# A transformer stack on one core: four plain inner tiles per feed-forward stage instead of six, and the paired blocks' input operands in another order and partly on GpSimd

## The chip, the cores and the metric

The kernel runs on one core of one Trainium2 chip. The metric is the device time of one execution in microseconds (us); the kernel before has a median of 1789.67 us over 3 runs (1787.99 to 1789.96). TensorE (PE) multiplies, VectorE (DVE), ScalarE (ACT) and GpSimd (POOL) work on tiles in SBUF, and SP issues the loads.

## What is computed

The reference runs a convolution layer, an attention layer and then one larger block on a sequence of 512 tokens with 1024 channels, all in float32. The change touches only the two feed-forward stages of the larger block (the "passes" below, one before its mixer and one after):

```python
def swiglu_ffn(x, g, w_gate, w_up, w_down):
    h = rms_norm_2(x, g)                      # x * rsqrt(mean(x*x) + eps) * g
    return (jax.nn.silu(h @ w_gate) * (h @ w_up)) @ w_down
x = x + 0.5 * swiglu_ffn(...)                 # D_MODEL = 1024, D_FF = 2816
```

## The kernel before

**Numbers.** Activations lie transposed: 8 tiles of 128 channels by 512 tokens (`k.xT`). Each float32 matrix is split into a rounded part ("hi", made on ScalarE) and a rest ("lo", the difference, made on VectorE or GpSimd), and a product is three matmuls: hi by hi, hi by lo, lo by hi. `mm3` (L262) does this, on L264 to L266. One `mm3` followed by one `tick()` is the unit of pacing.

**Weights.** `Stream` loads 512 KB granules in the order of use through 4 raw buffers (`RBUFS`), splits them into 6 pairs of hi and lo buffers (`WBUFS`), and does so as far ahead as buffers allow (`fill`, after each `done`). L100 makes the hi on ScalarE; L102 the rest, on GpSimd for the keys in `POOL_MORE` (L510) and for most parts of the sums below, on VectorE otherwise.

**The norm.** The 1/rms factor of a token isn't known when the first product starts. The products run on the tiles times gain, and the evictions from PSUM multiply by `rB`, the factor broadcast over all partitions. `Norm.stats1` (L361) sums the squares with small matmuls (L365), a short chain over VectorE and GpSimd makes four diagonal tiles (L392), and `stats2` spreads them by matmuls (L403) and copies the result to SBUF on ScalarE (L405). `a_group` calls it after k = `STATS_AT` = 4 of the 8 contraction steps, and `stats2` is put off by `STATS` = 6 ticks.

**The feed-forward stage** (`ffn`, L1513). Its 22 inner tiles of 128 columns fall into parts of 6, 4, 6 and 6, each followed later by its share of the down product. The first `FFN_PLAIN` = 6 inner tiles are plain: 8 `mm3` of 512 columns for the gate and 8 for the up matrix. Tiles 0 and 1 go first, as one group of four products with the contraction outermost; `e1` evicts (L1525, L1528) and applies SiLU, `e2` multiplies and splits (L1536, L279). The other tiles go in pairs: `seven` (L1599) computes a pair's product with seven half-size products of 256 columns in place of eight, from sums and differences of weight quarters (`split_sums`, L104: L117, L118, L126, L127) and of input quarters, and puts the results together with additions (L1615). `two` does this for gate and up.

**The input's operands.** `turn_x` (L1566) makes the seven input operands for the pairs, each in two halves j: it scales the input by gain and `rB` into quarters b11, b12, b21, b22 (L1578, sixteen instructions of 256 columns), takes the differences t1 = b12 - b11, t2 = b22 - t1, t3 = b22 - b12 and t4 = t2 - b21 (L1584, L1585, L1589, L1590), and splits all seven with `split_into` (hi on ScalarE L278, rest on VectorE L279). `seven` reads them in the order b11, b21, t2, t1, t3, b22, t4. `turn_x` is a side job: `tick()` gives it `TURN_RATE` = 0.5 units, and it gives up units at each `yield`; it is added after the first group, waits for `rB`, and must be through before the first pair.

**Order.** Each engine runs its instructions in one order, which is fixed when the program is built: a list scheduler takes instructions by their place in the program, and later ones earlier where the first aren't ready by its own reckoning.

## Time and profile before

| | |
|---|---|
| median of 3 runs | 1789.67 us |
| profiled execution: time, span | 1790.32 us, 1788.4 us |
| TensorE busy, of the span | 1750.5 us, 98% |
| VectorE, ScalarE, GpSimd busy | 1268.3 us, 892.3 us, 646.3 us |
| matmuls of 512 and of 256 columns on each of L264, L265 and L266 (inputs by streamed weights) | 1344 and 896 |
| granted TensorE clock, mean | 0.991 |

A busy time counts an instruction from its start to its end, waiting for a shared resource included; it is not work done. A matmul's recorded length overlaps the next one's, so its pace is read from starts. An engine's idle time is marked in a timeline in brackets, with what ended it.

### The profile page before, as it was taken

Reading aid. Unit: us, or ns where it says so; the run is one execution under the profiler, and the core shown is the slowest. Engines: PE = TensorE matmul, PEld = TensorE weight load, DVE = VectorE, ACT = ScalarE, POOL = GpSimd, SP = SyncE. Lnnn points to the kernel's source line nnn. Section 1 sums busy time; section 2 is a strip of 40 time slices with the busy share of each in tenths; the row PEclk is TensorE's granted clock in tenths of the full one; section 3 lists DMA queues with packets and bytes.
Section 4 is the critical chain, followed back from the end, with each engine's and each line's share of the span. In section 5 each row is a group of like instructions: output and inputs, shape, how many; then the busy total and the mean of one; then the engine's idle time right before and its main releaser. Section 6 shows DMA issues by size and latency. Waiting matters only on the chain.

```text
span 1788.4 us, 25274 instructions
## 1 busy us (share of the span) xinstructions
PE 1750.5 (98%) x9468; PEld 1488.6 (83%) x9468; DVE 1268.3 (71%) x2380; ACT 892.3 (50%) x1551; POOL 646.3 (36%) x418
## 2 busy tenths in 40 slices
PE   7999799999999999999999999899999999999999
PEld 5877588888888888889999888678888888899897
DVE  5999777565466667977676659997446569777872
ACT  5777545384636544434343435667643325344441
POOL 3999410302020003466675501000000044666662
PEclk8999899999999999999999999999999999999999
DMA  6422233131322232242342533113133321433432
GB/s 180 118 83 83 59 95 95 49 99 54 97 82 73 70 94 76 61 124 84 106 128 79 157 105 106 36 47 95 59 116 97 94 80 48 121 95 95 130 88 66
DMA packets 262758, 162.14 MB, mean 91 GB/s; under 512 B 10256, under 2 KB 245100, under 8 KB 262636
## 3 DMA queue, kind: packets, MB, share of 16 engines
q1 hardware_dynamic: 262636, 160.53, 30.8%
q8 instruction: 74, 1.21, 0.3%
q14 instruction: 48, 0.39, 0.1%
HBM read 155.23 MB, written 5.28 MB: 90 GB/s over the span
## 4 chain that ended last, share of the span: by engine, by line
PE 86%; DVE 2%; ACT 1%; issue 0%; POOL 0%; ACTq 0%; POOLq 0%
PE b L265 26%; PE b L264 26%; PE b L266 26%; PE b L1271 1%; PE b L1328 1%; PE b L1914 1%; PE b L1308 1%; PE b L1215 1%; PE b L2110 0%; PE b L1898 0%; PE b L1044 0%; PE b L1045 0%; PE b L403 0%; DVE wlo L102 0%; PE b L365 0%
## 5 line engine op out<-in xcount | busy, mean ns | idle before, releaser
L265 PE MATMUL b<-s,whi 128*128 128x512 f32 (+1 forms) x2240 | 789.5, 352 | 0.2
L264 PE MATMUL b<-s,whi 128*128 128x512 f32 (+1 forms) x2240 | 786.7, 353 | 2.5 <-ACT s L623 1.3
L266 PE MATMUL b<-s,wlo 128*128 128x512 f32 (+1 forms) x2240 | 786.9, 351 | 0.0
L102 POOL TENSOR_TENSOR wlo<-raw,whi 128x1024 fp32r<-128x1024 f32 (+2 forms) x163 | 337.7, 2088 | 420.5 <-ACT whi L100 382.4
L264 PEld LDWEIGHTS b<-s,whi 128*128 128x128 f32 x2240 | 422.9, 189 | 64.2 <-ACT s L860 2.2
L265 PEld LDWEIGHTS b<-s,whi 128*128 128x128 f32 x2240 | 423.1, 189 | 62.7 <-issue 2.4
L266 PEld LDWEIGHTS b<-s,wlo 128*128 128x128 f32 x2240 | 423.0, 189 | 61.1 <-issue 1.4
L100 ACT ACTIVATE whi<-raw 128x1024 fp32r<-128x1024 f32 (+2 forms) x304 | 285.3, 950 | 355.4 <-PE b L265 207.2
L102 DVE TENSOR_TENSOR wlo<-raw,whi 128x1024 fp32r<-128x1024 f32 (+1 forms) x141 | 179.5, 1277 | 38.9 <-ACT whi L100 32.3
L264 PE MATMUL b<-whi,s 128*128 128x512 f32 (+1 forms) x416 | 172.1, 415 | 0.0
L265 PE MATMUL b<-wlo,s 128*128 128x512 f32 (+1 forms) x416 | 168.6, 406 | 0.0
L266 PE MATMUL b<-whi,s 128*128 128x512 f32 (+1 forms) x416 | 164.6, 396 | 0.0
L100 ACT ACTIVATE whi<-s 128x512 fp32r<-128x512 f32 x128 | 77.2, 627 | 153.6 <-DVE s L127 74.0
L702 POOL TENSOR_TENSOR s<-s,s 128x512 f32<-128x512 f32 x88 | 128.3, 1489 | 3.2 <-ACT s L698 2.1
L1615 DVE TENSOR_TENSOR s<-b,s 128x256 f32<-128x256 f32 x192 | 76.1, 419 | 42.4 <-PE b L266 21.5
L102 POOL TENSOR_TENSOR wlo<-s,whi 128x512 fp32r<-128x512 f32 x64 | 98.2, 1555 | 20.8 <-ACT whi L100 15.2
L704 DVE SCALAR_TENSOR_TENSOR b<-s,s,b 128x512 f32<-128x512 f32 x144 | 99.9, 749 | 3.7 <-ACT b L692 2.9
L259 POOL TENSOR_TENSOR h8y<-hv,mhalf 128x8 f32<-128x8 f32 x28 | 47.4, 1694 | 131.4 <-DVE hv L1061 113.9
L279 DVE TENSOR_TENSOR s<-s,s 128x512 fp32r<-128x512 f32 x84 | 87.5, 1064 | 5.9 <-ACT s L278 5.6
L266 PEld LDWEIGHTS b<-whi,s 128*128 128x128 f32 x416 | 79.2, 190 | 13.9
L264 PEld LDWEIGHTS b<-whi,s 128*128 128x128 f32 x416 | 79.2, 190 | 12.4 <-ACT s L1837 0.2
L265 PEld LDWEIGHTS b<-wlo,s 128*128 128x128 f32 x416 | 79.2, 191 | 10.9
(434 smaller groups left out, 2086.6 us busy)
## 6 DMA issues: line engine op xcount, KB each, us to landing
raw<-in_ffn_w_gate SPq DMA_DIRECT2D x44, 512.0 KB
raw<-in_ffn_w_up SPq DMA_DIRECT2D x44, 512.0 KB
raw<-in_attn_w_in SPq DMA_DIRECT2D x40, 512.0 KB
raw<-in_ffn_w_down SPq DMA_DIRECT2D x48, 384.0 KB
raw<-in_w_in SPq DMA_DIRECT2D x36, 512.0 KB
raw<-in_conv_w_in SPq DMA_DIRECT2D x24, 512.0 KB
raw<-in_ple_w_gate SPq DMA_DIRECT2D x16, 512.0 KB
raw<-in_conv_w_out SPq DMA_DIRECT2D x8, 512.0 KB
```

The source lines that it names most:

```text
L100: self.last_hi = self.k.nc.scalar.activation(hi, src, AF.Copy)
L102: eng.tensor_tensor(lo, src, hi.bitcast(F32), OP.subtract)
L259: self.nc.gpsimd.tensor_tensor(y, v, self.mhalf[:, :shape], OP.pow)
L264: mm(ps, a[0], b[0], start=first, stop=False)
L265: mm(ps, a[0], b[1], start=False, stop=False)
L266: self.last = mm(ps, a[1], b[0], start=False, stop=last)
L279: nc.vector.tensor_tensor(lo, src, hi.bitcast(F32), OP.subtract)
L702: nc.gpsimd.tensor_tensor(acc2, acc2, p, OP.add)
L704: nc.vector.scalar_tensor_tensor(acc, y[:, t:t + S], wcol(t, c), acc, OP.mult, OP.add)
L1215: nc.tensor.transpose(pt[:, j * 128:(j + 1) * 128], w[:, j * 128:(j + 1) * 128], k.ident)
L1271: nc.tensor.matmul(ps[:, i * w + kb * 128:i * w + kb * 128 + 128], Q[g, b][:, hc], kk[h % 2][:, hc], start=True, stop=True)
L1615: add = lambda out, p, q, op=OP.add: V.tensor_tensor(out, p, q, op)
```

## The change

The plain inner tiles are 4 instead of 6, so that each pass has nine pairs instead of eight, and the first pair comes right after tiles 0 to 3. `a_group` takes the step after which it calls its hook, and `ffn` passes 3 instead of 4; the second half of the norm's statistics is put off by 4 ticks instead of 6 there. `turn_x` is added before the first group instead of after it, with a rate of 0.55, and goes in the order in which `seven` reads: b11 and b21 of both halves first, then t1 and t2, then t3, b22 and t4. A new `split_x` makes the rests of b11, b21, b22 and t4 on GpSimd; those of t1, t2 and t3 stay on VectorE. `POOL_MORE` follows `FFN_PLAIN`: of the plain tiles, the weights of 2 and 3 have their rests on GpSimd, where it was 2 to 5.

```diff
--- before.py
+++ after.py
@@ -306,7 +306,7 @@
         assert k == nk
         return ps
 
-    def a_group(self, X, keys, hook=None):
+    def a_group(self, X, keys, hook=None, at=None):
 
         pss = [self.ps.get() for _ in keys]
         gs = [self.W.take(kk) for kk in keys]
@@ -315,7 +315,7 @@
             for ps, g in zip(pss, gs):
                 self.mm3(ps, self.wpart(g, k * 128), X[k], k == 0, k == nk - 1)
                 self.tick()
-            if hook and k == STATS_AT:
+            if hook and k == (STATS_AT if at is None else at):
                 hook()
         for g in gs:
             self.W.done(g)
@@ -372,9 +372,9 @@
         self.dg = diagonals(k, self.r4)
         k.behind = self.k.last_diag
 
-    def stats(self):
+    def stats(self, n=None):
         self.stats1()
-        self.k.defer(STATS, self.stats2)
+        self.k.defer(n or STATS, self.stats2)
 
     def stats2(self):
         self.rB = self.k.spread(self.r4, self.dg)
@@ -471,7 +471,7 @@
 
 
 FFN_PARTS = (6, 4, 6, 6)
-FFN_PLAIN = 6
+FFN_PLAIN = 4
 
 
 def ffn_order():
@@ -1502,6 +1502,8 @@
 X_ACT, X_DVE = 4, 6
 STATS = 6
 STATS_AT = 4
+STATS_FFN = 4
+STATS_FFN_AT = 3
 TURN = 9
 TURN_M = 10
 LAG = (1, 3, 5)
@@ -1568,31 +1570,56 @@
 
         while not hasattr(nm, "rB"):
             yield 0.2
+        q = {}
+
+        def quarter(kh, th, j):
+            t = q[kh, th, j] = mem.get()
+            for e in range(2):
+                n = 4 * kh + 2 * j + e
+                V.scalar_tensor_tensor(t[:, e * 256:(e + 1) * 256], k.xT[n][:, th * 256:(th + 1) * 256],
+                                       k.col(nm.gain, nm.at + n), nm.rB[:, th * 256:(th + 1) * 256], OP.mult, OP.mult)
+
+        for kh in range(2):
+            for j in range(2):
+                quarter(kh, 0, j)
+                TX[("b11", "b21")[kh], j] = split_x(q[kh, 0, j])
+                yield 0.9
+        t1, t2 = {}, {}
         for j in range(2):
-            q = {}
-            for kh in range(2):
-                for th in range(2):
-                    t = q[kh, th] = mem.get()
-                    for e in range(2):
-                        n = 4 * kh + 2 * j + e
-                        V.scalar_tensor_tensor(t[:, e * 256:(e + 1) * 256], k.xT[n][:, th * 256:(th + 1) * 256],
-                                               k.col(nm.gain, nm.at + n), nm.rB[:, th * 256:(th + 1) * 256],
-                                               OP.mult, OP.mult)
-                    yield 0.8
-            b11, b12, b21, b22 = (q[x] for x in ((0, 0), (0, 1), (1, 0), (1, 1)))
-            t1, t2 = mem.get(), mem.get()
-            V.tensor_tensor(t1, b12, b11, OP.subtract)
-            V.tensor_tensor(t2, b22, t1, OP.subtract)
-            yield 1.4
-            TX["t2", j] = k.split_into(t2)
+            quarter(0, 1, j)
+            yield 0.8
+            t1[j] = mem.get()
+            V.tensor_tensor(t1[j], q[0, 1, j], q[0, 0, j], OP.subtract)
+            mem.put(q.pop((0, 0, j)))
             yield 0.7
+            quarter(1, 1, j)
+            yield 0.8
+            t2[j] = mem.get()
+            V.tensor_tensor(t2[j], q[1, 1, j], t1[j], OP.subtract)
+            yield 0.7
+            TX["t2", j] = k.split_into(t2[j])
+            yield 0.7
+            TX["t1", j] = k.split_into(t1[j])
+            mem.put(t1[j])
+            yield 0.7
+        for j in range(2):
+            b12, b21, b22 = (q.pop((*x, j)) for x in ((0, 1), (1, 0), (1, 1)))
             V.tensor_tensor(b12, b22, b12, OP.subtract)
-            V.tensor_tensor(t2, t2, b21, OP.subtract)
-            yield 1.4
-            for name, t in (("b11", b11), ("b21", b21), ("t1", t1), ("t3", b12), ("b22", b22), ("t4", t2)):
-                TX[name, j] = k.split_into(t)
-                mem.put(t)
-                yield 0.7
+            yield 0.7
+            TX["t3", j] = k.split_into(b12)
+            TX["b22", j] = split_x(b22)
+            yield 0.8
+            V.tensor_tensor(t2[j], t2[j], b21, OP.subtract)
+            TX["t4", j] = split_x(t2[j])
+            mem.put(b12, b21, b22, t2[j])
+            yield 0.8
+
+    def split_x(t):
+
+        hi, lo = mem.get(F32R), mem.get(F32R)
+        nc.scalar.activation(hi, t, AF.Copy)
+        nc.gpsimd.tensor_tensor(lo, t, hi.bitcast(F32), OP.subtract)
+        return hi, lo
 
     halves2 = slice(0, 256), slice(256, 512)
 
@@ -1695,10 +1722,11 @@
                 mem.put(nm.rB)
             two(j)
         elif i == 0:
-            p4 = k.a_group(X, [("fg", l, 0), ("fu", l, 0), ("fg", l, 1), ("fu", l, 1)], nm.stats)
+            turn = k.add_side(turn_x(), TURN_RATE)
+            p4 = k.a_group(X, [("fg", l, 0), ("fu", l, 0), ("fg", l, 1), ("fu", l, 1)],
+                           lambda: nm.stats(STATS_FFN), STATS_FFN_AT)
             k.defer(0, lambda: e1(0, p4[0], p4[1]))
             k.defer(0, lambda: e1(1, p4[2], p4[3]))
-            turn = k.add_side(turn_x(), TURN_RATE)
             i += 1
         else:
             pg = k.a_tile(X, ("fg", l, j))
@@ -1707,7 +1735,7 @@
         i += 1
 
 
-TURN_RATE = 0.5
+TURN_RATE = 0.55
```

## Rows read from the trace of the kernel before

**Rows 1.** The page: engine totals, and by line the chain that ended last.

```profile
PE 1750.5 (98%) x9468; PEld 1488.6 (83%) x9468; DVE 1268.3 (71%) x2380; ACT 892.3 (50%) x1551; POOL 646.3 (36%) x418
...
PE b L265 26%; PE b L264 26%; PE b L266 26%; PE b L1271 1%; PE b L1328 1%; PE b L1914 1%; PE b L1308 1%; PE b L1215 1%; PE b L2110 0%; PE b L1898 0%; PE b L1044 0%; PE b L1045 0%; PE b L403 0%; DVE wlo L102 0%; PE b L365 0%
```

**Rows 2.** Stages of the first pass: stretch, length, busy PE PEld DVE ACT POOL, clock, DMA.

```profile
683.00:752.50 69.50, 69.50 (x307) 56.15 (x307) 57.20 (x79) 29.37 (x44) 27.16 (x11) 1.00 0.23 65
752.50:772.30 19.80, 19.80 (x170) 19.80 (x169) 15.58 (x24) 10.86 (x19) 12.03 (x7) 1.00 0.23 68
868.00:927.40 59.40, 59.40 (x505) 59.40 (x504) 44.63 (x77) 28.61 (x50) 38.51 (x24) 1.00 0.34 97
```

**Rows 3.** The same view, from the scale's arrival to the last operand, both passes.

```profile
706.40:753.00 46.60, 46.60 (x203) 37.46 (x202) 46.55 (x61) 22.90 (x34) 22.92 (x9) 1.00 0.27 76
1451.50:1500.40 48.90, 48.90 (x221) 39.76 (x221) 48.81 (x61) 23.76 (x36) 25.47 (x10) 1.00 0.25 73
```

**Rows 4.** TensorE's timeline at stage borders: start, length, line, operands. Both passes.

```profile
705.50 0.48 PE L265 MATMUL b<-s,whi 128*128 128x512 f32 x1
...
752.48 0.28 PE L264 MATMUL b<-s,whi 128*128 128x256 f32 x1
...
772.29 0.39 PE L264 MATMUL b<-s,whi 128*128 128x512 f32 x1
...
1450.53 0.48 PE L266 MATMUL b<-s,wlo 128*128 128x512 f32 x1
...
1497.86 0.28 PE L264 MATMUL b<-s,whi 128*128 128x256 f32 x1
...
1517.75 0.39 PE L264 MATMUL b<-s,whi 128*128 128x512 f32 x1
```

**Rows 5.** VectorE's timeline: last sums of squares, and the last operand split.

```profile
693.22 0.68 DVE L358 TENSOR_TENSOR s<-s,s 128x512 f32<-128x512 f32 x1
...
752.98 0.68 DVE L279 TENSOR_TENSOR s<-s,s 128x512 fp32r<-128x512 f32 x1
...
1432.80 0.68 DVE L358 TENSOR_TENSOR s<-s,s 128x512 f32<-128x512 f32 x1
```

**Rows 6.** Timelines of TensorE and ScalarE around the norm's scale.

```profile
698.56 0.48 PE L266 MATMUL b<-s,wlo 128*128 128x512 f32 x1
...
704.69 1.05 PE L403 MATMUL b<-diag,ones 128*128 128x128 f32 x8
...
705.78 0.60 ACT L405 ACTIVATE s<-b 128x512 f32<-128x512 f32 x1 [0.25 <-PE b L403]
...
711.08 0.61 ACT L278 ACTIVATE s<-s 128x512 fp32r<-128x512 f32 x1
...
1450.94 0.58 ACT L405 ACTIVATE s<-b 128x512 f32<-128x512 f32 x1
```

**Rows 7.** Timelines of VectorE and GpSimd in the plain stage.

```profile
705.61 10.05 POOL L102 TENSOR_TENSOR wlo<-raw,whi 128x1024 fp32r<-128x1024 f32 x4 [5.62 <-ACT whi L100]
...
707.02 0.68 DVE L1528 TENSOR_TENSOR s<-b,s 128x512 f32<-128x512 f32 x1
707.62 8.72 DVE L1578 SCALAR_TENSOR_TENSOR s<-s,pc,s 128x256 f32<-128x256 f32 x5
...
716.86 2.45 DVE L1578 SCALAR_TENSOR_TENSOR s<-s,pc,s 128x256 f32<-128x256 f32 x6
...
719.82 2.74 POOL L102 TENSOR_TENSOR wlo<-raw,whi 128x1024 fp32r<-128x1024 f32 x1 [4.16 <-ACT whi L100]
719.83 3.01 DVE L1578 SCALAR_TENSOR_TENSOR s<-s,pc,s 128x256 f32<-128x256 f32 x2
...
735.20 1.88 DVE L279 TENSOR_TENSOR s<-s,s 128x512 fp32r<-128x512 f32 x3
```

**Rows 8.** Rests on GpSimd, by line: durations ns min/median/max. First 684 us; 845 to 927.

```profile
L102 POOL TENSOR_TENSOR wlo<-raw,whi x20: 2343/2414/2864, 15.0 to 678.8; 128x1024 fp32r<-128x1024 f32 x20
...
L102 POOL TENSOR_TENSOR wlo<-s,whi x12: 1281/1298/1752, 857.9 to 915.5; 128x512 fp32r<-128x512 f32 x12
```

## The prediction

> **What bounds the kernel now.** I read the engine totals and the chain that ended last, then the stages of the feed-forward passes, then the engines that feed TensorE there. TensorE is busy 98% and the chain runs over its three split-product lines, 26% each [rows 1]. In the pass it is busy for every microsecond of each stage, at a granted clock of 1.00, the 2.4 GHz level [rows 2]; so a matmul that goes is time that goes, as long as nothing new makes TensorE wait. In the plain stage VectorE is nearly as full: from the moment the norm's scale arrives until the last operand of the paired blocks is split it is busy 46.55 of 46.6 us, and 48.81 of 48.9 in the second pass [rows 3]. That is a second bound, just hidden: its last split of an operand starts at 752.98, and the block that multiplies these operands starts at 752.48 [rows 4, 5].
>
> **Fewer matmuls: the gain.** Two plain tiles are 2 tiles x 2 matrices x 8 x 3 = 96 matmuls of 512 columns. From 705.50 to 752.48 stand 9 + 192 = 201 of them, so 46.98/201 = 0.2337 us each and 22.44 for the 96; a paired block (2 x 7 x 4 x 3 = 168 matmuls of 256 columns) ran from 752.48 to 772.29 = 19.81 [rows 4]. Gain 2.63. In the second pass 47.33/202 x 96 = 22.49 against 19.89: 2.60 [rows 4]. Together 5.2 us. That is the whole prize: steady blocks are already TensorE-bound (three in a row take 59.4 us, TensorE busy 59.40 [rows 2]). Weight traffic I cost at nothing: each of the 22 tiles still loads two 512 KB granules through the same four raw buffers, SP only issues some sooner, and in three blocks in a row no load held TensorE up; the one place without that cover is the new block's second half, whose loads must follow tile 3's splits by 710 and are wanted some 30 us later.
>
> **The scale sooner.** The sum of squares is taken after k = 3, not 4: four times three matmuls, 12 x 0.234 = 2.8 us. The data allow it: the last square is added at 693.22, the statistics' matmuls end by 698.56 and would end by 695.8; in the second pass the last square is 18 us ahead of the scale [rows 5, 6]. The shorter deferral (4 ticks for 6, 1.4 us by its count) I cost at nothing: 6 ticks are 18 matmuls, yet 26 stand between statistics and broadcast (698.56 to 704.69 [rows 6]), so the written deferral isn't what places it. At most it gives 1.4 us more. So the scale stands at 706.38 - 2.8 = 703.6.
>
> **Less time for the operands.** The first paired block comes 22.44 us sooner, at 752.48 - 22.44 = 730.0. Its products take 19.81/14 = 1.415 us each: "b11" at 730.0, "b21" 731.5, "t2" 732.9, "t1" 734.3, "t3" 735.7, "b22" 737.1, "t4" 738.5, whose second half is read at 739.3. The new order delivers in that order, so the last ones decide. What VectorE must issue from 703.6 until "t4" can be split: 16 scaled quarters at 0.395 ((2.45 - 0.47)/5 from six in a row); at 0.60 ((1.88 - 0.68)/2 from three splits [rows 7]) 8 differences, 6 rests ("t2", "t1", "t3"), 4 weight sums and 2 weight rests of the block's first half, 6 evictions of tiles 0 to 2, 4 products and rests of tiles 0 and 1: 6.3 + 30 x 0.602 = 24.4 us.
>
> **What GpSimd costs VectorE.** GpSimd has in the same time 3 weight rests of 1024 columns (tile 3's two, the block's first), 2 of 512, and now 8 operand rests of 512. Alone these take 2.343 and 1.281 at least [rows 8]: 3 x 2.343 + 10 x 1.281 = 19.8 us. They aren't free. While a GpSimd rest runs, a VectorE instruction that reads two SBUF tensors stands still: five quarters took 8.72 beside four rests, and two took 3.01 beside one, where six took 2.45 beside none; one that reads PSUM passed in 0.68 [rows 7]. The size comes from the plain stage of before: 61 instructions, 16 x 0.395 + 45 x 0.602 = 33.4 us of work, took 46.55, so 13.1 were lost beside GpSimd work of 7 x 2.343 + 2 x 1.281 = 19.0; the second pass lost 15.4 beside 20.2 [rows 3, 8]. That is 0.69 to 0.76 us per GpSimd microsecond. I take it for the new rests too. No rest of an operand stands on GpSimd before; the bounds are 0 (all of them beside PSUM reads) and 1 (none), and the nearest rows, weight rests of the same size, took 1.28 to 1.75 [rows 8]; I take 1.28, as the excess is waiting already counted. So a rest moved away frees 0.60 on VectorE and takes 0.88 to 0.97: eight cost about 2.6 us a pass instead of freeing 4.8.
>
> The Trainium skill's page "SBUF — State Buffer", section "Who interferes with whom", says that a VectorE instruction with two SBUF inputs contends with a GpSimd instruction that reads SBUF, and the later one blocks fully. By that rule the loss would be 1 per microsecond and the time that of rival 3; the trace agrees on who blocks whom, and the stage's mixture gives 0.7.
>
> **The sum.** 703.6 + 24.4 + 19.8 x (0.69 to 0.76) = 741.7 to 743.1; the last operand's copy on ScalarE (0.61 [rows 6]) and the uncounted part of its own rest add about 1: 742.7 to 744.1 against 739.3. "t4" is 3.4 to 4.8 late. Second pass: scale at 1451.52 - 2.8 = 1448.7 [rows 6], need at 1497.86 - 22.49 + 9.3 = 1484.7, ready at 1448.7 + 24.4 + 15.1 + 1 = 1489.2: 4.5 late. Behind it in GpSimd's queue is the first weight rest of the block's second half (2.34), wanted 1.4 after the last product starts: with its start, another 1.5. Then the remaining work (3.6 us of VectorE, 3.8 of GpSimd, products of tiles 2 and 3) has the 9.9 us of seven products and no longer ends last. Lost per pass 5.7, gained 2.6: net +3.1, twice, +6.2. The profiled execution took 1790.3 (span 1788.4 and 1.9 around it), so 1796.5; the median of the runs shown lies 0.65 lower: **1796**.
>
> Other edits cost nothing: an eviction of tile 0 may stand behind operand work in VectorE's queue, covered because its PSUM bank is next written by the block at 730; tile 3's weight rests stand behind four operand rests on GpSimd, 705 + 4 x 1.28 + 2 x 2.4 = 715, wanted at 730.0 - 11.2 = 718.8, and without that cover TensorE would wait there. The rate of 0.55 ends the issuing some 9 ticks before the block, so pace isn't the limit.
>
> **Rivals.** (1) *The whole gain, faster.* GpSimd's rests fall beside PSUM reads, and VectorE's old order was the waste: the work ends at 703.6 + 24.4 + 1 = 729, before 739.3, nothing is late, 1789.7 - 5.2 = 1784.5. It decides where the loss per GpSimd microsecond is under (739.3 - 729)/19.8 = 0.52. For it: in three blocks in a row VectorE (44.63 us busy) and GpSimd (38.51) work side by side without delaying TensorE [rows 2]; against it: 0.69 and 0.76 in this very stage. (2) *A wash.* Loss of 0.55 to 0.65, or the scale 1.4 us sooner and the second half's weights on time: 1 to 4 us late per pass, 1787 to 1793. (3) *Full blocking.* 703.6 + 24.4 + 19.8 + 1 = 748.8 is 9.5 late, with 1.5 behind it 11: net +8.4 twice, 1806. For it: VectorE issues in order, so one blocked instruction holds the evictions behind it; against it: PSUM reads did pass. (4) *The scale isn't sooner*, because the matmuls of the statistics are placed later again: 2.8 more per pass, 1801.6.
>
> **Chances.** This kernel's measurement tells 0.2% (3.6 us) from no change. Forecast (1793.3 to 1800) 0.43, full blocking or a scale that isn't sooner (1800 to 1808) 0.17, wash 0.18, whole gain 0.22. So faster 0.22, same 0.18, slower 0.60. The range reaches from the whole gain's time, rounded to 1785, to just short of full blocking, 1805; the likeliest case's own is 1793 to 1800.
>
> **What would show it.** Right: 64 fewer 512-column and 112 more 256-column matmuls on each product line; the first quarter near 703.6; TensorE idle within 20 us after its first 256-column matmul, released by GpSimd's operand rests or by VectorE, some 5 us a pass; quarters stretched to 1.6 or 2.6 us. Wrong: TensorE without a gap where plain tiles give way to blocks, or GpSimd rests beside unstretched VectorE work.

## The result: 1.25% slower, and the profile after

The changed kernel takes 1811.15 us (median of four runs, 1810.0 to 1814.13) against 1789.11 for the kernel before in the same comparison: a ratio of 1.0125, interval 1.0109 to 1.0141. The forecast was 1796, slower; the direction was right, the size was not. The profiled execution took 1810.1 us, its span is 1808.3.

First the page of the changed kernel: the engine totals, which answer to [rows 1], and TensorE's first product line with its shapes (columns: busy us, mean ns, idle time before it and what ended most of it).

```profile
PE 1755.8 (97%) x9612; PEld 1498.9 (83%) x9612; DVE 1286.9 (71%) x2408; ACT 897.9 (50%) x1571; POOL 687.9 (38%) x442
...
L265 PE MATMUL b<-s,whi 128*128 128x512 f32 (+1 forms) x2288 | 799.9, 350 | 13.1 <-POOL s L1621 9.3
```

TensorE has more instructions, as intended, but its busy time did not fall (1750.5 before), and 9.3 us of idle time wait for GpSimd's L1621: that is the new helper's rest of an operand. TensorE's timeline at the borders of the stages shows where, as in [rows 4] (start, length, line, operands):

```profile
701.39 1.05 PE L403 MATMUL b<-diag,ones 128*128 128x128 f32 x8
...
725.72 0.28 PE L264 MATMUL b<-s,whi 128*128 128x256 f32 x1
...
781.14 0.39 PE L264 MATMUL b<-s,whi 128*128 128x512 f32 x1
...
1454.93 1.05 PE L403 MATMUL b<-diag,ones 128*128 128x128 f32 x8
...
1483.37 0.28 PE L264 MATMUL b<-s,whi 128*128 128x256 f32 x1
...
1537.89 0.40 PE L264 MATMUL b<-s,whi 128*128 128x512 f32 x1
```

From 725.72 to 781.14 stand two paired blocks. Two such blocks take 2 x 19.81 = 39.6 us in [rows 4]; here they take 55.4, and 54.5 instead of 39.8 in the second pass: **15.8 and 14.7 us lost**, together 30.5, against the 5.2 us that the plain tiles give back. Later blocks and all down products run without a wait. (30.5 - 5.2 is more than the 19.9 us between the two spans: the kernel's first spread of a norm's scale on L403, long before the changed code, stands at 204.0 us here and at 208.2 before; in the other profiles of this study it lies between 199.7 and 207.6.)

The waits of TensorE in these stretches, from its timeline (the bracket: idle time before it, and what ended it):

```profile
732.21 0.58 PE L265 MATMUL b<-s,whi 128*128 128x256 f32 x1 [3.35 <-DVE s L279]
...
741.77 0.38 PE L265 MATMUL b<-s,whi 128*128 128x256 f32 x1 [1.42 <-POOL s L1621]
745.12 0.58 PE L265 MATMUL b<-s,whi 128*128 128x256 f32 x1 [2.38 <-POOL s L1621]
747.38 0.79 PE L264 MATMUL b<-s,whi 128*128 128x256 f32 x2 [0.81 <-ACT s L1620]
...
1493.08 0.39 PE L264 MATMUL b<-s,whi 128*128 128x256 f32 x1 [2.12 <-ACT whi L100]
...
1496.63 0.58 PE L264 MATMUL b<-s,whi 128*128 128x256 f32 x1 [2.09 <-ACT s L1620]
1499.86 0.58 PE L265 MATMUL b<-s,whi 128*128 128x256 f32 x1 [2.65 <-POOL s L1621]
1505.63 0.58 PE L265 MATMUL b<-s,whi 128*128 128x256 f32 x1 [2.84 <-POOL s L1621]
```

With three smaller ones these are 9.1 us of idle time in the first pass and 9.9 in the second. The other 6.7 and 4.8 us are not idle time. Most of them shows in the view by stretches (length, busy PE PEld DVE ACT POOL with counts, granted clock, DMA):

```profile
706.40:753.00 46.60, 38.47 (x193) 33.43 (x192) 41.47 (x55) 19.84 (x32) 36.96 (x17) 0.85 0.17 49
...
732.30:737.00 4.70, 4.54 (x20) 4.25 (x21) 3.46 (x6) 0.00 (x0) 4.70 (x2) 0.50 0.00 0
745.20:750.00 4.80, 3.99 (x17) 3.69 (x18) 4.80 (x8) 3.66 (x6) 2.83 (x3) 0.50 0.00 0
760.00:770.00 10.00, 10.00 (x87) 10.00 (x86) 9.86 (x17) 5.06 (x9) 6.41 (x4) 1.00 0.28 79
```

Behind a wait the granted clock is 0.50, the 1.2 GHz level: 20 matmuls in 4.7 us, one every 0.213, where the steps at 1.00 are 0.118 (87 in 10 us). Some 50 and 31 matmuls of the two passes ran so; at 0.095 each that is 4.7 and 2.9 us. The rest stands at the edges of the waits: the first step behind one is up to 0.38, and the bracket counts only from the recorded end of the matmul before. The first line is the stretch of [rows 3]: VectorE, full before, has 5 us to spare, and GpSimd has gone from 22.9 to 37.0 us busy, over 10 of them the lengthening of a single rest (11.92 us, shown further down). The last operands now end on GpSimd.

### The profile page after: what moved, and what is told of

The parts are those of the page before. It is cut to its first block, busy times and chain, and to the rows that moved or that the text cites. A ratio compares the mean times of both kernels' runs of the same rounds, so it can differ in the third digit from the quotient of the medians.

```text
span 1808.3 us, 25674 instructions
## 1 busy us (share of the span) xinstructions
PE 1755.8 (97%) x9612; PEld 1498.9 (83%) x9612; DVE 1286.9 (71%) x2408; ACT 897.9 (50%) x1571; POOL 687.9 (38%) x442
## 3 DMA queue, kind: packets, MB, share of 16 engines
q8 instruction: 75, 1.23, 0.3%
## 5 line engine op out<-in xcount | busy, mean ns | idle before, releaser
L265 PE MATMUL b<-s,whi 128*128 128x512 f32 (+1 forms) x2288 | 799.9, 350 | 13.1 <-POOL s L1621 9.3
L264 PE MATMUL b<-s,whi 128*128 128x512 f32 (+1 forms) x2288 | 796.7, 350 | 7.5 <-ACT s L1620 2.9
L266 PE MATMUL b<-s,wlo 128*128 128x512 f32 (+1 forms) x2288 | 796.4, 348 | 1.2 <-DVE wlo L102 1.2
L265 PEld LDWEIGHTS b<-s,whi 128*128 128x128 f32 x2288 | 435.6, 190 | 74.1 <-POOL s L1621 10.3
L102 POOL TENSOR_TENSOR wlo<-raw,whi 128x1024 fp32r<-128x1024 f32 (+2 forms) x163 | 342.8, 2118 | 397.2 <-ACT whi L100 344.2
L264 PEld LDWEIGHTS b<-s,whi 128*128 128x128 f32 x2288 | 435.9, 191 | 66.8 <-ACT s L1620 3.4
L266 PEld LDWEIGHTS b<-s,wlo 128*128 128x128 f32 x2288 | 435.9, 191 | 59.3 <-DVE wlo L102 1.6
L100 ACT ACTIVATE whi<-raw 128x1024 fp32r<-128x1024 f32 (+2 forms) x304 | 283.0, 943 | 342.1 <-PE b L265 210.5
L102 DVE TENSOR_TENSOR wlo<-raw,whi 128x1024 fp32r<-128x1024 f32 (+1 forms) x141 | 179.2, 1274 | 37.5 <-ACT whi L100 31.1
L100 ACT ACTIVATE whi<-s 128x512 fp32r<-128x512 f32 x144 | 86.1, 626 | 155.4 <-DVE s L127 83.1
L102 POOL TENSOR_TENSOR wlo<-s,whi 128x512 fp32r<-128x512 f32 x72 | 111.7, 1571 | 14.0 <-ACT whi L100 14.0
L1642 DVE TENSOR_TENSOR s<-b,s 128x256 f32<-128x256 f32 x216 | 85.6, 418 | 42.3 <-PE b L266 21.6
L117 DVE TENSOR_TENSOR s<-raw 128x512 f32<-128x512 f32 x36 | 45.2, 1257 | 65.9 <-DMA raw<-in_ffn_w_gate 39.2
```

The source lines that it names most:

```text
L100: self.last_hi = self.k.nc.scalar.activation(hi, src, AF.Copy)
L102: eng.tensor_tensor(lo, src, hi.bitcast(F32), OP.subtract)
L117: V.tensor_tensor(s1, B[:, one], B[:, two], OP.add)
L264: mm(ps, a[0], b[0], start=first, stop=False)
L265: mm(ps, a[0], b[1], start=False, stop=False)
L266: self.last = mm(ps, a[1], b[0], start=False, stop=last)
```

## The experiments

Times are medians; each ratio is to the kernel before, run beside it on the same chip. "Waits" are TensorE's idle times in the first two paired blocks, first and second pass, from each kernel's trace.

```
kernel                                    us       ratio [interval]           waits
changed kernel                            1811.15  1.0125 [1.0109, 1.0141]    9.1  9.9
e1 eight rests on VectorE                 1804.02  1.0089 [1.0074, 1.0104]    6.0  8.0
e2 six plain tiles, rest of the change    1796.54  1.0044 [1.0027, 1.0060]    3.0  1.7
e3 eight rests' work left out             1792.86  1.0027 [1.0017, 1.0037]    6.7  0.7
e4 nothing of the stage on GpSimd         1801.05  1.0073 [1.0056, 1.0090]    7.1  4.9
e5 four plain tiles and nothing else      1810.19  1.0128 [1.0113, 1.0143]    7.6  9.6
e6 down product between, old order        1799.87  1.0067 [1.0053, 1.0081]    4.2  5.4
e7 a fifth raw buffer                     1817.26  1.0161 [1.0144, 1.0178]   11.3 10.3
e8 changed kernel with filler matmuls     1813.10  1.0140 [1.0123, 1.0157]    6.0  3.6
e9 down product of two tiles between      1820.78  1.0174 [1.0159, 1.0190]    0.0  0.4 (and 6.9, 4.3 ahead of them)
e10 down between, new order, VectorE      1804.07  1.0093 [1.0078, 1.0108]    3.0  2.2 (and 5.9, 0.2 ahead)
```

### m1: the two engines side by side

A kernel of its own: rows of 18 VectorE instructions beside GpSimd ones.

> The disputed resource by itself; the kernel computes none of the reference. Seven stretches, each started on both engines by one ScalarE copy: 6 GpSimd differences of 512 columns alone; 18 VectorE differences of two SBUF tiles alone; both; 18 scaled quarters (256 columns, two SBUF tiles and a column) with the 6; 18 VectorE differences that read PSUM with the 6; every fourth of the 18 from PSUM with the 6; 18 differences with 6 GpSimd fills that read nothing. Theory A (GpSimd reads and VectorE's two-SBUF-input instructions exclude each other, and a gapless run of VectorE differences isn't interrupted): alone 6 x 1.28 = 7.7 us and 18 x 0.60 = 10.8 us; both together 18.5, with the first GpSimd difference recorded as some 10 us long; quarters take turns with GpSimd, one quarter to one difference, 18 x 0.395 + 6 x 1.28 = 14.8 in all; beside PSUM reads no loss, 10.8; every fourth from PSUM: GpSimd gets in at the PSUM reads, one rest at each, 13 to 16; beside fills 10.8. Theory B (no exclusion, only too much work on VectorE): each pair of streams takes the longer of the two, 10.8, and no instruction is longer than alone.

Timelines of VectorE and GpSimd: the row of two-operand subtractions (28.95), and that of subtractions that read PSUM (66.11), each beside six rests:

```profile
28.95 18.38 DVE L46 TENSOR_TENSOR vo<-g,y 128x512 f32<-128x512 f32 x18 [0.69 <-ACT g L67]
28.99 10.10 POOL L58 TENSOR_TENSOR go<-g,y 128x512 f32<-128x512 f32 x6 [12.44 <-ACT g L67]
39.17 1.59 POOL L74 TENSOR_TENSOR b<-go,g 128x512 f32<-128x512 f32 x1
...
66.11 10.86 DVE L52 TENSOR_TENSOR vo<-ps,g 128x512 f32<-128x512 f32 x18 [0.69 <-ACT g L67]
66.16 7.39 POOL L58 TENSOR_TENSOR go<-g,y 128x512 f32<-128x512 f32 x6 [6.90 <-ACT g L67]
```

Eighteen instructions that read PSUM take 10.86 us and lose nothing beside six rests; the same eighteen with two SBUF operands take 18.38 beside six rests and one more GpSimd addition. That is 7.5 us lost beside 7 x 1.26 = 8.8 of GpSimd: 0.85 for each microsecond, and GpSimd's rests go from 1.23 apart (7.39/6) to 1.68 (10.10/6). The Trainium skill's page "SBUF — State Buffer", section "Who interferes with whom", calls this an exclusive lock; the two engines taking strict turns here agree with it. What did not come out as I had it is that an unbroken VectorE row would keep GpSimd out: it got its turn each time, also with every fourth instruction from PSUM (17.2 us, where I had 13 to 16). The quarters took 14.35 us (I had 14.8). Two stretches are no clean comparison: the row "alone" (11.99 us) had one GpSimd addition beside it, and the fills ran before the row that they were meant for.

### m2: a rest that arrives in the middle of a row

In the changed kernel a single GpSimd weight rest took 11.92 us, until VectorE's row ended. This kernel tries that alone.

> A kernel of its own, which computes nothing of the reference: six stretches, in each twenty VectorE subtractions of 128x512 (two operands in SBUF) in an unbroken row, and GpSimd subtractions (rests) of the same size whose operand is a ScalarE copy of what the fourth, and in the fifth stretch also the ninth and the fourteenth, of the row wrote, so that they arrive when the row is already running. Theory A2 (whoever arrives in the middle of an overlapped VectorE row is held off until the row ends or is broken): in stretch 1 the single rest is recorded at about 10 us (the 15 remaining subtractions at 0.60 plus its own 1.27) and no VectorE subtraction takes over 0.7; in stretch 2 four rests make the first one 10 us and the others 1.3 to 1.7 behind the row; in stretch 3, whose thirteenth is a PSUM read, the rest gets in there, at about 6 us; in stretch 4, whose thirteenth is a fill (no operand in SBUF), at 6 us as well; in stretch 5 the first of the three rests takes 10 us and the other two follow behind the row; in stretch 6, where a rest begins before the row does, the two engines alternate from the start (1.7 each). Rival (the engines take turns whenever both want the port, as when they began together): a rest takes 1.7 to 1.9 wherever it arrives, the VectorE subtraction beside it 1.7, and no rest takes over 2.5; then the 11.92 us of the kernel have another cause than the row.

```profile
4.10 8.17 DVE L44 TENSOR_TENSOR vo<-g,y 128x512 f32<-128x512 f32 x10
...
7.27 1.58 POOL L53 TENSOR_TENSOR go<-h,y 128x512 f32<-128x512 f32 x1 [6.83 <-ACT h L71]
```

All eight arrivals got in behind the VectorE instruction that was running (1.51 to 1.59 us each). Theory A2 is refuted as a general rule. The long holds of the kernel traces are real, and I could not produce one alone.

### e1 and e3: who does the eight rests

```
-        nc.gpsimd.tensor_tensor(lo, t, hi.bitcast(F32), OP.subtract)
+        nc.vector.tensor_tensor(lo, t, hi.bitcast(F32), OP.subtract)      # e1
+        nc.scalar.activation(lo, t, AF.Copy)                              # e3
```

> The changed kernel with the eight operand rests back on VectorE, all else as changed. Theory A: eight rests of 1.28 on GpSimd that cost VectorE up to as much, and that wait through its runs, become 8 x 0.60 = 4.8 us on VectorE a pass; TensorE's idle time at the first pairs falls from 15.8 and 14.7 us to about 5 a pass, time about 1794. Theory B (VectorE's own work doesn't fit into 22 us less): VectorE has 4.8 us more per pass, the idle time grows to about 20 a pass, time about 1820.

> The changed kernel with the eight operand rests left out: a second copy on ScalarE stands in each one's place, so the operands b11, b21, b22 and t4 are wrong. No rest on GpSimd and none on VectorE. Theory A: both blockades go, with only the weights' rests left on GpSimd; TensorE idle under 4 us a pass, time about 1787 to 1790. Theory B (VectorE's own queue is the limit): VectorE's work is the same as in the changed kernel, idle stays above 10 us a pass, time above 1803.

e3 replaces the eight rests by second copies, so its operands' low parts are not the reference's. Both runs came out between the times of their two theories. GpSimd's rests cost 0.98% against e3 (17.5 us), VectorE's 0.62% (11 us; 16 x 0.60 = 9.6 us of instructions). So the work seems to be in one account for both engines, and it is cheaper on VectorE. But even without the eight rests nothing is gained, and the two passes part. In the second the two blocks take 41.1 us, 1.3 over steady ones, and the gain is nearly kept. In the first they lose 10.0, with as little work to do, by the same way as in the changed kernel (see the step that failed, below): a GpSimd weight rest takes 11.93 us from 722.28, VectorE's L117 stands 5.06 us for a load behind it (to 738.11), and TensorE for a copy behind that:

```profile
742.36 0.50 PE L264 MATMUL b<-s,whi 128*128 128x256 f32 x2 [4.64 <-ACT s L1620]
```

### e2 and e5: the change taken apart

```
 FFN_PLAIN = 6      # e2: in the changed kernel;   e5: FFN_PLAIN = 4 in the kernel before
```

> The changed kernel with six plain tiles again: order of use, rests on GpSimd, scale at k = 3 and the rate stay. Both theories: the operands have 22 us more, nothing is late, 1789 (1787 to 1792). If the new order or the rests cost time by themselves, whatever the room, TensorE would be idle at the first pair here too and the time over 1793.

> The kernel before with four plain tiles instead of six and nothing else of the change: order of operands, engines and statistics as before. Its first pair comes 22.4 us sooner than before, near 729 to 730 in the first pass, and needs first the b11 of both halves, whose rests end at 726 and at 732 to 736 in the trace of before. Theory A: the pair waits some 6 to 8 us at its first products and 2 to 5 at the later ones, so 8 to 12 a pass minus 2.6: 1800 to 1809, that is no worse than the changed kernel (1811), whose order gains and whose GpSimd rests lose. Rival (the order of use is worth what the prediction held, some 5 us a pass and more): 1815 or above.

Four plain tiles alone cost 1.28%, as much as the whole change. Everything else alone costs 0.44%, with six plain tiles and 22 us more room, by waits for GpSimd's weight rests (two of 1.83 and 1.16 us in the first pass). So the rest of the change saves, beside four plain tiles, about what its GpSimd rests cost, and no more: e1, which has the new order without these rests, is 0.39% below e5, and the rests on GpSimd add 0.36%. e5 came out 1 us above what theory A allowed (1800 to 1809), below the rival's 1815.

### e4: nothing of the stage on GpSimd

```
-            self.halves(p, slice(0, 1024), A, True)
+            self.halves(p, slice(0, 1024), A, pool)     # pool: not the first pair
...
-POOL_MORE = {(n, l, i) for n in ("fg", "fu") for l in (1, 2) for i in range(2, FFN_PLAIN)}
+POOL_MORE = set()
```

> All of the changed kernel, but in the feed-forward stages the eight operand rests, the weight rests of plain tiles 2 and 3 and those of the first pair of tiles are all VectorE's, so that GpSimd shares no port with it between the statistics and the first pair. Theory A (VectorE's row holds GpSimd's weight rests off, and with them raw buffers, the next load, and VectorE's own weight sum behind that load): with 8 rests on VectorE alone the kernel took 1804.0 and its passes stood 10.5 and 11.0 us; with nothing on GpSimd each pass stands under 5 us, and the time is 1787 to 1796. Rival B (VectorE simply has too much to do in 20 us): the weight rests, some 8 us more of VectorE's time a pass, come on top of the 21.5 us of stalls, and the time is 1810 to 1820.

Between the two, and not above e1, although VectorE has some 8 us more a pass to do. By stretches of its trace:

```profile
707.90:736.50 28.60, 25.20 (x128) 20.87 (x127) 28.60 (x54) 15.30 (x25) 0.00 (x0) 1.00 0.19 54
```

GpSimd is empty, VectorE issues its instructions without a pause, and TensorE waits 3.14 us at 736.02 for one of them (L279). Nothing is held off: in this stretch it is VectorE's quantity. Order plays a part all the same: the last difference ended at 740.18, and the last operand rest began at 749.82, behind evictions, products and weight sums in VectorE's own queue. In the second pass TensorE waits for no operand at all, though VectorE makes them all; its 4.9 us there are waits for weights (2.29 us for L100, the rest nearly all for L102).

### e7: is it the raw buffer?

```
-RBUFS = 4
+RBUFS = 5
-SLOTS = 71
+SLOTS = 70
```

> The changed kernel with a fifth buffer for raw weights (and one arena slot less, for room). Theory D (in the first pass VectorE's weight sum stood 5.13 us at 735.76 to 740.90 for a load that had no free raw buffer, because the GpSimd weight rest that read the buffer took 11.92 us, and t4's second difference stood behind the sum): the load is there, the wait goes, the last operands come some 4 to 5 us sooner in the first pass; the second pass, whose last rest waited in GpSimd's own queue, gains nothing: 1804 to 1808. Rival (the buffer is not what t4 waits for; the sum or the rest would be late anyway): 1809 to 1814, with VectorE's idle time turned into another wait.

Theory D fell: the median is 6 us above the changed kernel's. The load's wait is gone, but VectorE stands 2.39 us at 730.25 for GpSimd's L1621 instead (and 2.40 at 1491.57 in the second pass), both times ahead of an eviction (L1530) that reads no operand rest, and TensorE waits as long elsewhere. (The profile is of an execution of 1810 us, the fastest of its four.) With one arena slot less it is no clean test, and these two waits may be for the missing slot; it shows that one more raw buffer is not enough.

### m3 and e8: the lower clock

> A kernel of its own, which computes nothing of the reference: eight streams of 120 matmuls of 256 columns (two operands of 128 partitions, fp32r), each of which waits for a chain of VectorE and ScalarE copies that begins with the result of the stream before; the chain is 0, 0, 1, 2, 3, 4, 5 and 7 copies longer, so the waits grow from about 1.2 to 4 us. Theory: in the changed kernel the matmuls behind the waits of 3.35, 2.38 and 0.81 us in the first pass stepped at 0.213 us instead of 0.118 at a granted clock of 0.50, because TensorE had stood still; then here too the matmuls behind the waits of about 2.4 us and more step at 0.213 for 15 to 30 of them (1.5 to 3 us on top of the wait), and those behind 1.2 us at 0.118. Rival (the slow steps come from operands or weights that arrive slowly, not from the clock): every stream steps at 0.118 from its first matmul on, whatever its wait.

TensorE's timeline (streams of 120 equal matmuls, each behind a wait), and the stretches of 3.5 us behind two of the waits:

```profile
87.08 14.66 PE L48 MATMUL ps<-b,a 128*128 128x256 f32 x120 [2.76 <-ACT b L45]
104.95 16.15 PE L48 MATMUL ps<-b,a 128*128 128x256 f32 x120 [3.21 <-ACT b L45]
125.21 16.14 PE L48 MATMUL ps<-b,a 128*128 128x256 f32 x120 [4.11 <-ACT b L45]
```

```profile
87.08:90.58 3.50, 3.50 (x29) 3.50 (x30) 0.00 (x0) 0.00 (x0) 0.00 (x0) 1.00 0.00 0
104.95:108.45 3.50, 3.50 (x19) 3.50 (x20) 0.00 (x0) 0.00 (x0) 0.00 (x0) 0.62 0.02 5
```

Behind 2.76 us of standing still the clock is at 1.00 and 29 matmuls go in 3.5 us; behind 3.21 it is 0.62 on average and 19 go, and the stream is 1.5 us longer (16.15 against 14.66), as behind 4.11. I had expected it from about 2.4 us on. (The first stream, at the start of the program, was slow as well, 16.44 us.) All other operands were long there: the standing still does it.

e8 keeps TensorE busy where it would wait in the changed kernel:

```
+                if i0 == FFN_PLAIN and which == 0 and (name, kk) in PAD:
+                    to = y[:, R] if name == "t2" else w[:, R]
+                    for _ in range(PAD[name, kk]):
+                        nc.tensor.matmul(to, *old, start=True, stop=True)
...
+PAD = {("t2", 0): 12, ("b22", 0): 12, ("b22", 2): 16, ("t4", 0): 18}
```

> The changed kernel with 58 matmuls of 256 columns more in each pass, all in the first pair's first matrix and all into a half of a PSUM bank that nothing reads: 12 before the product of t2, 12 before that of b22, 16 before its second half, 18 before that of t4, which is where TensorE stood in the changed kernel. They do nothing but keep TensorE busy where it would wait (58 x 0.118 = 6.8 us, inside waits of 9.1 and 9.9 us). Theory C (behind its long waits TensorE ran at a granted clock of 0.50, and what it lost there, 0.095 us a matmul, is on top of the operands' lateness): no wait stays over 2.8 us and no stretch at 0.50, the operands come when they came; of the 49 and 32 slow steps only those behind the last late operand had counted, some 20 in each pass, so the time falls by 2 to 4 us: 1807 to 1809.5, with the matmuls behind the last wait at 0.118. Rival (the slow steps are not of the standing still, or the clock is not the filler's to keep): the steps behind the last wait stay at 0.213, and the filler costs up to its 6.8 us a pass: 1811 to 1825.

TensorE's timeline in its second pass (L1639 is the filler):

```profile
1505.81 3.81 PE L1639 MATMUL b<-s,whi 128*128 128x256 f32 x18
...
1510.91 0.39 PE L265 MATMUL b<-s,whi 128*128 128x256 f32 x1 [0.47 <-POOL s L1621]
```

In the second pass 16 slow matmuls are left of 31, 15 of them the filler's own and all ahead of the last wait, and the two blocks took 52.9 us instead of 54.5, 6.8 us of filler included; the 1.6 us agree with the 17 slow steps that had stood behind the last wait (17 x 0.095). In the first pass 32 slow matmuls of 50 stayed, another wait of 2.48 us came at 753.6, and the blocks took 56.5 instead of 55.4. The time is the changed kernel's within the intervals. So both theories fell short: the filler is free where it fits into the waits, the clock is worth 1.6 us in the second pass, and the first pass does not test it. A slow step ahead of a further wait only shortens that wait. What counts is when the last operand comes.

### e6, e9, e10: other work in between

```
-FFN_PARTS = (6, 4, 6, 6)
+FFN_PARTS = (3, 7, 6, 6)     # e6 with FFN_PLAIN = 4 in the kernel before; e10 in e1
+FFN_PARTS = (2, 8, 6, 6)     # e9 in e1
```

> The kernel before with four plain tiles, and with the parts of the feed-forward stage cut at 3, 7, 6, 6 tiles instead of 6, 4, 6, 6: the first down product (three tiles, 72 matmuls of 512 columns, 72 x 0.2337 = 16.8 us) then stands between the fourth plain tile and the first pair. Order of operands, engines and statistics as before. Theory A (the only fault of four plain tiles is that the first pair comes before its operands): the first pair comes 5.6 us sooner than in the kernel before, near 747, with operands due at 738.5 to 742: no stall or up to 2 us a pass, the 2.6 us a pass are kept, 1783 to 1788. Rival (weight rests on GpSimd come late beside VectorE's row, as with six plain tiles in the new order, 1796.5): 1790 to 1797. A third case, the down product waits for the gated output of its third tile or VectorE's eight additions hold the operands off: 3 to 6 us a pass, 1790 to 1796 as well, told apart by the releaser of TensorE's waits.

> Four plain tiles, the new order of operands, the eight rests on VectorE as in the second experiment, and the parts of the stage cut at 2, 8, 6, 6 tiles: the down product of the first two tiles (48 matmuls of 512 columns, 48 x 0.2337 = 11.2 us) comes behind the third plain tile, and the fourth plain tile (5.6 us) between it and the first pair. In the second experiment the last operand that TensorE waited for came at 739.6 in the first pass and at 1494.2 in the second (1504.5 counting the rest of the last difference); the first pair now comes 11.2 us later than there, near 740, and its last operand is wanted 8.5 us behind that. Theory A (operands due, nothing else): no stall in the first pass, 0 to 2 us in the second, and the 2.6 us a pass are kept: 1784 to 1789, faster than or level with the kernel before. Rival (the rest of the first pair's weights comes late, as in the run with parts of 3, 7, 6, 6, where VectorE's sums of the other matrix stood ahead of the rest that TensorE wanted: waits of 4.2 and 5.4 us): 1793 to 1800.

> Four plain tiles with the parts cut at 3, 7, 6, 6 as in the run with the down product between (16.8 us of it ahead of the first pair), but with the changed kernel's order of operands and the eight rests on VectorE. Theory A (the pair only came before its operands): the run with 2, 8, 6, 6 tiles had its pair at 742.1 and 1505.9 and no wait in it of over 0.5 us, but lost as much in its two-tile down product and in its eight-tile ones; with three and seven tiles these go (they cost nothing there in the run with the old order) and the pair stands 5 us later still: 1784 to 1790. Rival (the rests of the first pair's weights wait in VectorE's queue behind sums of the other matrix, as with the old order, whose waits of 4.2 and 5.4 us each cost 2 us more at the lower clock): 1795 to 1803.

None beats the kernel before, and no version here does; all three came out above even their rivals' ranges. In e6 the pair proper begins 42.4 us after the spread of the scale (701.27 to 743.62), finds its operands, and waits 4.2 and 5.4 us for one weight rest that stands in VectorE's queue behind sums of the other matrix. In e9 and e10 TensorE waits ahead of the pair. Their timelines, from the spread of the scale to the first matmuls of the pair proper (the scheduler had put two and four of its matmuls ahead of the last plain ones):

```profile
704.13 1.05 PE L403 MATMUL b<-diag,ones 128*128 128x128 f32 x8
...
722.01 2.93 PE L264 MATMUL b<-s,whi 128*128 128x512 f32 x6 [3.69 <-ACT s L278]
...
733.97 0.50 PE L265 MATMUL b<-s,whi 128*128 128x512 f32 x1 [3.22 <-DVE s L279]
...
752.76 0.28 PE L264 MATMUL b<-s,whi 128*128 128x256 f32 x1
```

```profile
703.70 1.05 PE L403 MATMUL b<-diag,ones 128*128 128x128 f32 x8
...
734.91 0.48 PE L264 MATMUL b<-s,whi 128*128 128x512 f32 x1 [2.03 <-ACT s L1622]
...
753.28 0.28 PE L264 MATMUL b<-s,whi 128*128 128x256 f32 x1
```

Between the scale and the pair e9 has 152 plain and down matmuls, 35.5 us at 0.2337, in 47.7. A down product that comes this early reads gated tiles, and these are made by the same VectorE queue as the operands (L278 and L279 are the two halves of the split helper). So the wait moved in front of the work that was to cover it, and in the first pass the pair begins 48.6 and 49.6 us after the scale's spread, where the kernel before had it at 47.8 (704.69 to 752.48). Further waits came behind the two blocks of the table, all for weights: 3.3 and 2.4 us in the next pairs of e9, 2.4 and 1.7 in those of e10, and 3.0 in each eight-tile down product of e9. My expectations for e9 and e10 looked only at the pair.

## Why the prediction was wrong, step by step

**The gain** held: the plain tiles are gone and steady blocks run at their old pace.

**The scale sooner** failed in the first pass: between L403 and the first paired matmul stand 24.3 us (701.39 to 725.72) where the step has 28.1 (730.0 less 704.69 - 2.8). The statistics were placed later again (rival 4), which takes 3.8 us of the operands' room. In the second pass it held: 28.4.

**VectorE's work** was counted right, its price was not. The step has 46 instructions, 24.4 us, up to "t4"; up to and with its last difference (L1612) the trace has 46 in the first pass and 40 in the second. From the first quarter to the end of that difference the sum has 38.1 to 39.5 us. The trace has 42.5 in the first pass (703.71 to 746.22), 5.13 of it a wait for a load, and 34.1 in the second (1456.65 to 1490.72). A microsecond of GpSimd cost more than the 0.69 to 0.76 taken: in the first unbroken row (703.71 to 735.76, 41 instructions, 21.4 us of work) 10.7 us were lost beside GpSimd's two rests of 1024 columns and six of 512, which alone take 12.4: 0.86, as in m1. The total came out lower only because the other rests did not run in that row; they came behind it.

**The step that failed** is the sum's last term: "the last operand's copy on ScalarE (0.61) and the uncounted part of its own rest add about 1". From the end of the last difference to the end of the last rest it measured 5.4 us in the first pass (746.22 to 751.63) and 14.9 in the second (1490.72 to 1505.58). In the first pass a second term failed with it, the weight traffic, put at nothing: it made VectorE wait those 5.13 us ahead of "t4"'s second difference. The timelines of GpSimd and then of VectorE and the load queue:

```profile
724.99 11.92 POOL L102 TENSOR_TENSOR wlo<-raw,whi 128x512 fp32r<-128x512 f32 x1 [6.52 <-ACT whi L100]
736.86 1.28 POOL L1621 TENSOR_TENSOR s<-s,s 128x512 fp32r<-128x512 f32 x1
738.10 2.40 POOL L102 TENSOR_TENSOR wlo<-raw,whi 128x1024 fp32r<-128x1024 f32 x1
...
749.90 1.73 POOL L1621 TENSOR_TENSOR s<-s,s 128x512 fp32r<-128x512 f32 x1
...
1494.11 2.36 POOL L102 TENSOR_TENSOR wlo<-raw,whi 128x1024 fp32r<-128x1024 f32 x1 [2.26 <-issue]
1496.42 3.39 POOL L1621 TENSOR_TENSOR s<-s,s 128x512 fp32r<-128x512 f32 x2
...
1503.93 1.65 POOL L1621 TENSOR_TENSOR s<-s,s 128x512 fp32r<-128x512 f32 x1 [2.43 <-DVE s L279]
```

```profile
703.71 15.44 DVE L1579 SCALAR_TENSOR_TENSOR s<-s,pc,s 128x256 f32<-128x256 f32 x12 [6.12 <-ACT s L405]
...
735.08 0.68 DVE L1612 TENSOR_TENSOR s<-s,s 128x512 f32<-128x512 f32 x1
740.90 1.37 DVE L117 TENSOR_TENSOR s<-raw 128x512 f32<-128x512 f32 x1 [5.13 <-DMA raw<-in_ffn_w_gate]
...
745.54 0.68 DVE L1612 TENSOR_TENSOR s<-s,s 128x512 f32<-128x512 f32 x1
...
1456.65 3.51 DVE L1579 SCALAR_TENSOR_TENSOR s<-s,pc,s 128x256 f32<-128x256 f32 x6 [5.54 <-ACT s L405]
...
1489.54 1.18 DVE L1612 TENSOR_TENSOR s<-s,s 128x512 f32<-128x512 f32 x1
...
1503.17 0.68 DVE L279 TENSOR_TENSOR s<-s,s 128x512 fp32r<-128x512 f32 x1
...
724.95 12.34 SPq L73 DMA_DIRECT2D raw<-in_ffn_w_gate  x2
```

The sum treats what GpSimd does as a tax on VectorE and gives GpSimd no lateness of its own. In the first pass GpSimd's weight rest is held from 724.99 to the end of VectorE's row; the raw buffer that it reads stays taken, so SP's second load is issued 12 us late; VectorE's weight sum (L117) stands 5.13 us for that load (with a fifth buffer, in e7, this wait was gone), and "t4"'s second difference, behind it in the same queue, comes at 745.54. In the second pass the differences are done by 1490.7 and the copies on ScalarE by 1496.6, but two rests stand in GpSimd's queue behind a weight rest, and the last one, with GpSimd idle for 2.43 us, waits by the profile for VectorE's split at 1503.17 (L279), which makes neither of its two inputs. That it waited for a buffer to come free is likely, but no run shows it. Measured from the first quarter to the last rest, the operands' way is 703.71 to 751.63 = 47.9 us, and 1456.65 to 1505.58 = 48.9: as long as the 46.6 and 48.9 of [rows 3]. The prediction had it at some 40. The first pair came some 22 us sooner and its operands did not: the second half of "t4" was wanted 9.3 us into the pair, at 735.0 and 1492.7, and TensorE's last wait for it ended at 747.38 and 1505.63, so it was 12.4 and 12.9 us late, not 3.4 to 4.8; with the slow clock this made the 15.8 and 14.7 us lost, where the sum has 5.7. (In the first pass other matmuls had been put ahead of those that read the very last rest, which held nothing up.)

The hold and the queue are how it went in this trace, not why it must: e7 takes the load's wait away and e4 the hold and GpSimd's queue, and TensorE waits for VectorE or for weights instead. What most runs support as the cause is the quantity, both engines' work together: VectorE is full in e4, e3 has less to do and loses least, and every experiment that brought the pair forward, whatever engine made its operands, lost. Six plain tiles hid the operands' way with nothing to spare. But quantity is not shown to be the only cause. e3's first pass loses 10.0 us by the hold and the load where its second loses 1.3; e4's second pass waits for no operand; and in e4's first pass, as in the second pass here, rests come long after their differences are done. No run changes the order within VectorE's queue by itself or adds buffers beside the raw ones, so whether another order would fit four plain tiles stays open.

**Not in the sum at all** is the 1.2 GHz level behind the waits, 4.7 and 2.9 us on the face of the trace; e8 shows it to be worth 1.6 in the second pass.

**The rivals.** Full blocking (1806) was nearest, and the 0.85 of m1 and 0.86 of the row stand nearer to its 1 than what I took, but its mechanism, a blocked VectorE, is not what ended last; that its time was near is in part luck. The whole gain and the wash are refuted. Rival 4 was half true, in the first pass alone. What I said would show it did: idle time released by GpSimd's operand rests, and quarters stretched (twelve took 15.44 us from 703.71); it was 9 to 10 us a pass, not 5.

## What to carry to other kernels

Where a second engine is full behind the bound one [rows 3], work taken from the bound engine is not a gain until the second one's work shrinks as well: look at how long the way to the last operand is, not at how much work is on it. Where work goes to another in-order queue, sum up that queue on its own, with what stands ahead of the last instruction and what each instruction holds (a raw buffer, and by it a load). Where the two engines take turns, as in m1, moving work between them moved most of the wait (e1 and e4 gave back 0.36 and 0.52 of the 1.25%); leaving eight rests out (e3) gave back 0.98.

## What the hardware showed that I had not expected

A GpSimd rest of 512 columns, 1.28 us alone, took 11.92 us in the changed kernel's first pass and 5.91 in its second, and 11.93 in e3; one of 1024 took 13.27 in e1 (2.40 alone). Each got in when the VectorE row broke off (735.76 in the changed kernel) or came to an instruction that reads PSUM (1488.93 there). In m1 and m2 instructions of the same shapes took turns from the first. What decides between the two stays open. And TensorE's clock behind a wait: in m3 no loss after 2.76 us, 1.5 us after 3.21 and also after 4.11; in the changed kernel it was slow behind 2.38 as well, with a wait of 1.42 shortly before.
